# Output projection in four groups of 512 columns with seven-product steps, and two weight sums as one operation

## The chip, the cores and the metric

The kernel runs on one core of a Trainium2 chip. The metric is the device time of one execution in microseconds (us). PE is the matrix engine, DVE the vector engine (VectorE), ACT the scalar engine (ScalarE), POOL GpSimd, SP the queue that issues most loads.

## What is computed

One layer of an encoder for 256 tokens with 2048 features: a gated linear attention mixer, its output projection, a squared-ReLU MLP and a last normalization. Cut to what matters here:

```python
h = x
o = ...                                   # attention, normalized by head, 256 x 2048
h = h + (o * silu(r)) @ w_out             # w_out 2048 x 2048: the output projection
a = relu(rmsnorm(h, mlp_norm) @ w_up)     # w_up 2048 x 8192
h = h + (a * a) @ w_down                  # w_down 8192 x 2048
return rmsnorm(h, final_norm)
```

All inputs are float32.

## The kernel before

**Products in three terms.** Each float32 weight tile is loaded into `raw`, copied by ScalarE to a rounded part `hi` (float32r, L118, `copy_hi`), and VectorE subtracts that from the tile to give `lo` (L131 in `parts`, L165 in `weights`). The activations are kept in two parts in the same way (`oth` and `otl` for the mixer's output, `hh` and `hl` for h). A product is then hi x hi + hi x lo + lo x hi, three matmuls of 128x128 by 128x256. The tokens make two tiles of 128 (`NT` = 2).

**Buffers.** `hi` and `lo` come from five slots each, `raw` from six buffers. ScalarE and VectorE run ahead of PE until the slots are full, and then wait for PE to free one. PE, ScalarE and VectorE each take their instructions in order; the order within an engine is set when the program is built, by a planner that runs the kernel's own order and moves side work (`side`, `pump`) to given steps. `issue_after` pins one instruction behind another in that order.

**The output projection before** is two calls of `natural` (L176 is its matmul, through `halves`), one for each half of 1024 columns of w_out. A call has 16 steps, one for each 128 rows of w_out: one load of 128x1024, one `hi`, one `lo`, and 24 matmuls into four banks (two token tiles by two halves of 512). After a call `add_h` (L640) adds the banks to h.

**Transposes.** The mixer's output `on` and h are turned by PE in bursts of eight transposes of 128x128 (`turn`, L595), four feature tiles each; ScalarE (L600) and VectorE (L601) then take the two parts out of the banks. Bursts one and two of `on` lie in the pass before the projection, three and four in the projection's first half; one and two of h lie in its second half, three and four in the first steps of the MLP.

**Rows at another offset.** After each burst the next step uses rows whose first half lies at another offset in its buffer: `EVEN` = (5, 6) are the two feature tiles concerned, `place_o` gives their places, `xe` holds such copies of x, and `even_at` puts these two tiles at the steps behind the bursts. In the MLP, `even` names the steps whose weights have a gap between their halves (`gap` in `weights`).

**Steps by sums in the MLP.** The down projection works in steps of 256 rows by 512 columns. Split in 2x2 blocks, such a step needs eight block products, or seven of sums of blocks: `forms` makes eight blocks of the activations (four plain, S1 to S4 sums), and the weights' four blocks are replaced in `raw` by sums. One of the weight sums comes with the load: GpSimd's queue loads a block with an accumulating DMA (L938). Three operations of VectorE make the rest in place (L961, L962, L963). So a step has two lots of weights: the loaded blocks (L131, 768 columns) and the sums (L1002, 1024 columns). Four banks collect the products; `combine` (L1043) adds and subtracts them at the end. `by_sums` says which steps are done so: 112 of 120, the last eight loads of w_down aside.

**The order of PE.** In the MLP, `in_order` pins each lot of matmuls behind the one before it.

Of the kernel before, what the change touches and what calls it, by code (L numbers as in the profile page):

```python
# [68 lines left out]
def tile_gla_mlp(ctx, tc, x, xt, cols, w_vg, w_in, w_gate, w_out, w_up, w_down, final_norm, out):  # L69
# [516 lines left out]
                nc.scalar.activation(s, acc[t][c], AF.Silu, scale=r1[:, t : t + 1])  # L586
                nc.vector.tensor_tensor(on[:, t, lo : lo + 512], on[:, t, lo : lo + 512], s, op=ALU.mult)

    def turn(src, row, gain, q):

        bs = [aux_bank(), aux_bank()]
        for i in range(4):
            kt, b, o = 4 * q + i, bs[i // 2], i % 2 * T
            for t in range(NT):
                nc.tensor.transpose(b[:, o + t * P : o + (t + 1) * P], src[:, t, kt * P : (kt + 1) * P], ident)  # L595
        for i in range(4):
            kt, b, o = 4 * q + i, bs[i // 2], i % 2 * T
            s = b[:, o : o + T].rearrange("p (t s) -> p t s", t=NT)
            dh, dl = row(kt)
            nc.scalar.activation(dh, s, AF.Copy, scale=gain(kt))  # L600
            nc.vector.scalar_tensor_tensor(dl, s, gain(kt), dh.bitcast(F32), op0=ALU.mult, op1=ALU.subtract)  # L601
# [4 lines left out]
    oth, otl = (big.tile([P, KT * T + 192], F32R, tag="B", name="ot" + i) for i in "hl")  # L606

    def place_o(kt):
# [6 lines left out]
    def row_o(kt, t):  # L615
        o, d = place_o(kt)
        return [a[:, o + t * d : o + t * d + P] for a in (oth, otl)]

# [8 lines left out]
    side.extend(turns(on, turned_o, gain_o, 0))  # L627
# [5 lines left out]
    side.extend(turns(on, turned_o, gain_o, 2))  # L633
    hs = const.tile([P, NT, 4], F32, name="hs")

    def add_h(acc, c0):
        for c in range(2):
            for t in range(NT):
                lo = c0 + 512 * c
                nc.vector.tensor_tensor(h[:, t, lo : lo + 512], acc[t][c], h[:, t, lo : lo + 512], op=ALU.add)  # L640

    def ssq_h(c0):
        for t in range(NT):
            for c in range(2):
                lo = c0 + 512 * c
                sq = tmp.tile([P, 512], F32, tag="t512", name="sq", bufs=1)
                nc.scalar.activation(sq, h[:, t, lo : lo + 512], AF.Square, accum_out=hs[:, t, lo // 512 : lo // 512 + 1])

    acc = natural(row_o, rows(w_out, 0), G, HALF, order=even_at(2, 4))
    flush()  # L650
    add_h(acc, 0)
# [3 lines left out]
    turned_h = lambda kt: [a[:, kt, :].rearrange("p (t s) -> p t s", t=NT) for a in (hth, htl)]  # L655
    side.extend(turns(h, turned_h, g2, 0))
    side.append(lambda: ssq_h(0))
    acc = natural(row_o, rows(w_out, G), G, HALF, order=even_at(2, 4))
    flush()
    add_h(acc, G)  # L660
    r2 = const.tile([P, NT], F32, name="r2")

    def scale2():
        ssq_h(G)
# [6 lines left out]
    def scale2_row():  # L671

        b = psum_bank(others[-1], "row")
        for t in range(NT):
            d = free_work[:, t * P : (t + 1) * P]
            nc.vector.tensor_scalar(d, ident, r2[:, t : t + 1], None, op0=ALU.mult)
            nc.tensor.matmul(b[:, t * P : (t + 1) * P], ones, d, start=True, stop=True)
        nc.scalar.copy(r2row, b[:, :T])


    side.extend([nothing] * 2 + [lambda: turn(h, turned_h, g2, 2), scale2] + [nothing] * 4)
    side.append(lambda: (turn(h, turned_h, g2, 3), scale2_row()))

    S3, S1, S2, S4, A12, A11, A22, A21 = range(8)
    KP = MR // P // 2
    GROUPS = D // GT
# [21 lines left out]
    firsts, others = list(acc_free)[:2], list(acc_free)[2:]  # L711
    free = deque([*firsts, *aux_free, *others])

    @contextmanager
    def in_order():
        with ExitStack() as order:
            if ordered[0] and last_mm[0]:
                order.enter_context(tc.issue_after(last_mm[0]))
            yield
        last_mm[0] = newest[0]  # L720

    def matmul(o, x, w, first, last):
        newest[0] = nc.tensor.matmul(o, x, w, start=first, stop=last, skip_group_check=True).ins  # L723

    def up():
        ended = deque()
        n_steps = [0]

        def piece():

            if ended:
                with tc.issue_after(last_lo[0].ins), tc.issue_after(last_hi[0].ins):
                    ended.popleft()()

                if n_steps[0] == UPS:
                    last_end[0], last_sum[0] = (i or j for i, j in zip(newest_form, (last_end[0], last_sum[0])))

        for m in range(ROUNDS):
            for q in range(MR // GT):
                taken = [free.popleft() for _ in range(2)]  # L740
                acc = [psum_bank(i, "up") for i in taken]
                even = ((1, 4), (0,))[q] if m == 0 else (6,) if (m, q) in ((ROUNDS // 2 - 1, 0), (ROUNDS - 1, 1)) else ()
# [12 lines left out]

    def up_step(acc, c0, kp, even):

        w = pair_of(w_up, kp, c0, even)

        def products(i, n):
            for j in range(GT // P):
                k = 1 - j % 2
                o = acc[j // 2][:, k * T : (k + 1) * T]
                for a in ((hth, htl), (hth,))[n]:

                    matmul(
                        o, w[n][:, i, j * P : (j + 1) * P], a[:, 2 * kp + i],  # L770
                        kp == i == n == 0 and a is hth and j % 2 == 0, kp == KT // 2 - 1 and n == 1,
                    )

        for i in range(2):
            with in_order():
                products(i, 0)
            if 2 * kp + i < KT - 1:
                pump()
        yield

        with in_order():
            for i in (1, 0) if kp in even else (0, 1):
                products(i, 1)

# [37 lines left out]
    def forms(m, kp, s):  # L822
        f = form
        on_act(nc.scalar.activation(
            f[:, A12:].rearrange("p (t i) s -> p i t s", t=2), s.rearrange("p i (t s) -> p i t s", t=2), AF.Square
        ))
        if True in ways_of(m, kp):
            sub = lambda o, x, y: on_vector(nc.vector.tensor_tensor(o, x, y, op=ALU.subtract))
            sub(f[:, S3 : S1 + 1], f[:, A21:].to_broadcast([P, 2, P]), f[:, A11 : A22 + 1])
            sub(f[:, S2], f[:, A11], f[:, S1])  # L830
            sub(f[:, S4], f[:, A12], f[:, S2])

    def form_parts(m, kp, act):
        ways = ways_of(m, kp)
# [34 lines left out]
    two = lambda bank: bank.rearrange("p (f s) -> p f s", f=2)  # L869

    def begin(k, g):
        i = free.popleft()
# [19 lines left out]
    def down(passes):  # L892
# [7 lines left out]
        for n, (m, g) in enumerate(passes):  # L900
# [12 lines left out]
            for kp in range(KP):  # L913
# [3 lines left out]

                def products(n, these, w, banks=banks, last=last):

                    with in_order():  # L920
# [33 lines left out]
                if by_parts:  # L954
                    these = (P16, 0, at(A11), block(1)), (B32, T, at(A12), block(3)), (B32, 0, at(S4), block(2))
                    u = raw.rearrange("p (f s) -> p f s", f=4)
                    tt = nc.vector.tensor_tensor


                    with tc.issue_after(last_lo[0].ins):  # L960
                        tt(u[:, 2], u[:, 0], u[:, 2], op=ALU.add)  # L961
                        tt(u[:, 1], u[:, 2], u[:, 1], op=ALU.subtract)  # L962
                        last_sum[0] = tt(u[:, 3], u[:, 2], u[:, 3], op=ALU.add).ins  # L963
                else:
                    these = [
                        (k, 0, at(f[i]), block(2 * i, 2))
# [73 lines left out]
    def combine(g):  # L1040
# [4 lines left out]
        def put(t):  # L1045
# [139 lines left out]
```

## Time and profile before

| | |
|---|---|
| Median of three runs | 1048.59 us (1048.42 to 1048.8) |
| Profiled execution | 1048.66 us, span from first to last instruction 1046.9 us |
| Granted PE clock, mean | 0.999 |
| Pass before the projection, end | 287.7 us from the start of the span |
| Output projection | 287.7 to 378.6 us |
| MLP | 378.6 us to the end |

How to read the rows below. The page's first part gives each engine's busy time, share of the span and number of instructions. A row of windows has, for a stretch of time, each engine's busy time and (x) count of instructions, the granted clock of PE, the share of the DMA engines that was in use, and GB/s. A row of groups has line, engine, operation, output and inputs with shapes, count, busy time and mean duration in ns of one, then the engine's idle time before them and what ended it. A row of the timeline has start, time from the first start to the last end, engine, line, operation, and how many instructions were merged. PE's matmuls are pipelined: one lasts 0.28 us, but the next begins long before that.

### The profile page before, as it was taken

The numbers are of one execution on the slowest core, as the hardware profiler recorded it, in microseconds if no ns is written. First come the engines' busy times: TensorE is split into PE (matmuls) and PEld (weight loads), VectorE is DVE, ScalarE is ACT, GpSimd is POOL, SyncE is SP. The second block draws the span as 40 slices with busy tenths as digits, with TensorE's granted clock in tenths as the row PEclk, the third lists the DMA queues.
The fourth block names the chain that finished last, engine by engine and source line by source line (L and its number), as shares of the span: only waits on it lengthen the run. The fifth ranks groups of instructions, "written<-read, shape, count | busy, mean of one in ns | idle before, by whom it ended". The sixth has DMA issues, their size and how long they took to land. (4 is left out here: it accounts for less than half of the span.)

```text
span 1046.9 us, 23145 instructions
## 1 busy us (share of the span) xinstructions
PE 1038.5 (99%) x9094; PEld 1038.2 (99%) x9094; DVE 843.9 (81%) x1225; ACT 703.9 (67%) x1045; POOL 110.1 (11%) x151
## 2 busy tenths in 40 slices
PE   9999999999999999999999999999999999999997
PEld 9999999999999999999999999999999999999997
DVE  5768654656465566889999999999999999999887
ACT  6785544546455455678678678778778777777785
POOL 0000000010000001111111111121211111211100
PEclk9999999999999999999999999999999999999999
DMA  9957665556656666688888887888888888887772
GB/s 337 326 175 215 192 198 165 158 145 180 200 180 184 186 216 193 166 223 226 228 237 229 230 249 210 245 235 224 238 234 227 243 235 229 229 229 223 232 244 88
DMA packets 112717, 225.21 MB, mean 215 GB/s; under 512 B 10288, under 2 KB 25264, under 8 KB 112480
## 3 DMA queue, kind: packets, MB, share of 16 engines
q1 hardware_dynamic: 95808, 207.39, 63.8%
q0 software_dynamic: 16128, 14.69, 9.4%
q10 hardware_dynamic: 672, 1.66, 0.4%
q8 instruction: 71, 1.16, 0.4%
q14 instruction: 38, 0.31, 0.1%
HBM read 221.60 MB, written 2.10 MB: 214 GB/s over the span
## 5 line engine op out<-in xcount | busy, mean ns | idle before, releaser
L118 ACT CAST hi<-raw 128x768 fp32r<-128x768 f32 (+4 forms) x610 | 490.1, 846 | 280.5 <-PE acc L176 105.0
L131 DVE TENSOR_TENSOR lo<-raw,hi 128x768 fp32r<-128x768 f32 (+3 forms) x226 | 241.9, 1072 | 123.7 <-ACT hi L118 121.2
L723 PE MATMUL acc<-hi,act 128*128 128x256 f32 x1696 | 247.8, 276 | 0.0
L723 PE MATMUL up<-hh,hi 128*128 128x256 f32 x1024 | 238.9, 276 | 0.0
L723 PE MATMUL up<-hl,hi 128*128 128x256 f32 x1024 | 238.8, 276 | 0.0
L165 DVE TENSOR_TENSOR lo<-raw,hi 128x1024 fp32r<-128x1024 f32 x160 | 194.7, 1219 | 30.5 <-ACT hi L118 30.2
L723 PEld LDWEIGHTS acc<-hi,act 128*128 128x128 f32 x1696 | 217.7, 188 | 0.0
L723 PEld LDWEIGHTS up<-hl,hi 128*128 128x128 f32 x1024 | 192.2, 188 | 0.0
L723 PEld LDWEIGHTS up<-hh,hi 128*128 128x128 f32 x1024 | 192.2, 188 | 0.0
L938 POOL DMA_DIRECT2D raw<-in_w_down x112 | 98.3, 878 | 516.2 <-DMA raw<-in_w_down 208.0
L1002 DVE TENSOR_TENSOR lo<-raw,hi 128x1024 fp32r<-128x1024 f32 x112 | 136.4, 1218 | 1.6 <-ACT hi L118 1.0
L723 PE MATMUL up<-hh,lo 128*128 128x256 f32 x1024 | 137.0, 276 | 0.0
L723 PE MATMUL acc<-lo,act 128*128 128x256 f32 x848 | 134.0, 276 | 0.0
L723 PEld LDWEIGHTS up<-hh,lo 128*128 128x128 f32 x1024 | 125.7, 188 | 0.0
L723 PEld LDWEIGHTS acc<-lo,act 128*128 128x128 f32 x848 | 113.4, 188 | 0.0
L176 PE MATMUL acc<-hi,xA 128*128 128x256 f32 (+1 forms) x728 | 105.5, 279 | 0.0
L176 PEld LDWEIGHTS acc<-hi,xA 128*128 128x128 f32 x728 | 94.2, 189 | 0.1
L176 PE MATMUL acc<-lo,xA 128*128 128x256 f32 (+1 forms) x364 | 60.7, 278 | 0.0
L176 PEld LDWEIGHTS acc<-lo,xA 128*128 128x128 f32 x364 | 50.3, 188 | 0.0
L961 DVE TENSOR_TENSOR raw<-raw 128x256 f32<-128x256 f32 x112 | 47.4, 423 | 2.9
L962 DVE TENSOR_TENSOR raw<-raw 128x256 f32<-128x256 f32 x112 | 47.4, 423 | 2.8
L219 PE MATMUL acc<-xA,hi 128*128 128x256 f32 x288 | 49.2, 276 | 0.0
(159 smaller groups left out, 1201.2 us busy)
## 6 DMA issues: line engine op xcount, KB each, us to landing
raw<-in_w_up SPq DMA_DIRECT2D x128, 512.0 KB, 4.5
raw<-in_w_down SPq DMA_DIRECT2D x224, 256.0 KB, 4.5
raw<-in_w_in SPq DMA_DIRECT2D x80, 512.0 KB, 3.8
raw<-in_w_out SPq DMA_DIRECT2D x32, 512.0 KB, 3.7
raw<-in_w_down POOLq DMA_DIRECT2D x112, 128.0 KB, 5.2
raw<-in_w_down SPq DMA_DIRECT2D x16, 512.0 KB, 4.9
raw<-in_w_vg SPq DMA_DIRECT2D x14, 520.0 KB, 8.9
h<-in_x SPq DMA_DIRECT2D x4, 512.0 KB, 7.1
```

The lines of the kernel that those rows point to most:

```text
L118: last_hi[0] = nc.scalar.copy(to, raw)
L131: last_lo[0] = nc.vector.tensor_tensor(lo[:, s], raw[:, s], hi[:, s].bitcast(F32), op=ALU.subtract)
L165: last_lo[0] = nc.vector.tensor_tensor(to[1], dst, to[0].bitcast(F32), op=ALU.subtract)
L176: nc.tensor.matmul(o[:, m], x, w[:, m], start=first and c == 0, stop=last, skip_group_check=True)
L219: nc.tensor.matmul(o, u[:, i, s], m, start=kt == 0 and n == 0 and j % 2 == 0, stop=kt == KT - 1 and n == 2, skip_group_check=True,)
L723: newest[0] = nc.tensor.matmul(o, x, w, start=first, stop=last, skip_group_check=True).ins
L938: nc.gpsimd.dma_start(out=raw[:, :T], in_=src[:, 0, T:], accum_op=ALU.add)
L961: tt(u[:, 2], u[:, 0], u[:, 2], op=ALU.add)
L962: tt(u[:, 1], u[:, 2], u[:, 1], op=ALU.subtract)
L1002: last_lo[0] = nc.vector.tensor_tensor(to[1][:, :G], u, to[0][:, :G].bitcast(F32), op=ALU.subtract)
```

## The change

**The output projection** is done by a new function, `out_group`, for each of four groups of 512 columns, in eight steps of 256 rows, in the order of row pairs 3, 0, 2, 1, 4, 7, 5, 6. Pairs 0, 1 and 7 (`FORMED`) are done by sums as in the MLP, 12 steps of 32; the others in plain form, 24 matmuls each. For these three pairs `turn_pair` makes the eight blocks of activations, in two parts, from the transposed bank. The loads are two of 128x512 and one accumulating one for a step by sums, else one of 128x2x512. h is copied into a group's two banks ahead of it (`begin_out`), and two more banks collect sums; at a group's end, VectorE combines these in four operations (into `comb`) and writes h from the two banks and `comb`. The bursts three and four of `on` are done together, in group 0, burst n of h in group n for 1 to 3, all between the second and the third step of a group, ahead of pair 2; the last burst of h stays in the MLP. The rows at another offset are now those of pair 2 (`BOTH` = feature tiles 4 and 5). A second lot of matmuls of a step by sums (`pending`) comes after the next step's.

**Weight sums:** `weight_sums` makes them in two VectorE operations in place of three, the second over two blocks at once, in the projection and in the MLP. Signs differ, and those of the activations' sums (`form_sums`) and of `combine` follow; `form_sums` has three operations as before.

**Order:** `in_order` becomes `then_mm`, which pins PE's lots from the projection on, and in the MLP's first steps too.

The diff, cut to its core:

```diff
+    def form_sums(f, tt):
+        tt(f[:, S3], f[:, A21], f[:, A11], ALU.subtract)
+        tt(f[:, S2 : S1 + 1], f[:, A22 : A22 + 1].to_broadcast([P, 2, P]), f[:, 0::7], ALU.add)
+        tt(f[:, S4], f[:, A12], f[:, S2], ALU.subtract)
+
+    def weight_sums(u):
+        nc.vector.tensor_tensor(u[:, 2], u[:, 0], u[:, 2], op=ALU.subtract)
+        return nc.vector.tensor_tensor(u[:, 1::2], u[:, 1::2], u[:, 2:3].to_broadcast([P, 2, T]), op=ALU.subtract)
...
+    def turn_pair(kp, bank, gain, to):
+        raw_form = raw_forms[kp == 1]
+        for i in range(2):
+            s = bank[:, i * T : (i + 1) * T].rearrange("p (t s) -> p t s", t=NT)
+            nc.scalar.activation(raw_form[:, A12 + 1 - i :: 2], s, AF.Copy, scale=gain(2 * kp + i))
+        form_sums(raw_form, lambda o, x, y, op: nc.vector.tensor_tensor(o, x, y, op=op))
+        nc.scalar.copy(to[0], raw_form)
+        nc.vector.tensor_tensor(to[1], raw_form, to[0].bitcast(F32), op=ALU.subtract)
...
-        e = EVEN[0]
-        if kt in EVEN:
+        e = BOTH[0]
+        if kt in BOTH:
...
-    acc = natural(row_o, rows(w_out, 0), G, HALF, order=even_at(2, 4))
...
-    acc = natural(row_o, rows(w_out, G), G, HALF, order=even_at(2, 4))
...
+        for step, kp in enumerate(order):
+            by = kp in summed
+            raw = raw_tile()[:, : 2 * GT]
...
+            w = parts(raw, 2 * GT, slots(), [(T * by, 2 * GT)])
+            if by:
...
+                products([(p16, 0, at(A11), block(1)), (banks[0], T, at(A12), block(3)), (banks[0], 0, at(S4), block(2))], w)
+                u = raw.rearrange("p (f s) -> p f s", f=4)
+                with tc.issue_after(last_lo[0].ins):
+                    weight_sums(u)
+            else:
+                for t, i in ((0, 0), (0, 1), (1, 0), (1, 1)):
+                    products([(banks[t], 0, row_o(2 * kp + i, t), block(2 * i, 2))], w, step == len(order) - 1 and i == 1)
+            if pending:
+                pending()
+                pending = None
+            if step in between:
+                with tc.issue_after(last_hi[0].ins), tc.issue_after(last_lo[0].ins), then_mm():
+                    between[step]()
...
+    ORDER = (3, 0, 2, 1, 4, 7, 5, 6)
+    out_group(0, ORDER, FORMED, {
+        1: lambda: (turn(on, turned_o, gain_o, 2), turn(on, turned_o, gain_o, 3, forms_o, spare_out(0))),
+        3: lambda: begin_out(1),
+    })
...
+        out_group(g, ORDER, FORMED, {
+            1: lambda: turn(h, turned_h, g2, g - 1), 4: lambda: ssq_h(g - 1),
+            **({3: lambda: begin_out(g + 1)} if g + 1 < GROUPS else {}),
+        })
...
-                even = ((1, 4), (0,))[q] if m == 0 else ...
+                even = ((4,), (0,))[q] if m == 0 else ...
...
-                        tt(u[:, 2], u[:, 0], u[:, 2], op=ALU.add)
-                        tt(u[:, 1], u[:, 2], u[:, 1], op=ALU.subtract)
-                        last_sum[0] = tt(u[:, 3], u[:, 2], u[:, 3], op=ALU.add).ins
+                        last_sum[0] = weight_sums(u).ins
...
-            tt(2, 1, 2, ALU.subtract), tt(0, 0, 2, ALU.subtract), lambda: put(0),
-            tt(1, 2, 3, ALU.subtract), tt(0, 0, 3, ALU.add), lambda: put(1),
+            tt(2, 1, 2, ALU.add), tt(0, 0, 2, ALU.subtract), lambda: put(0),
+            tt(1, 2, 3, ALU.add), tt(0, 0, 3, ALU.subtract), lambda: put(1),
```

More of the change, by code (lines that the diff above doesn't have):

```diff
@@ L587, in gate_out, with turn @@
                 nc.vector.tensor_tensor(on[:, t, lo : lo + 512], on[:, t, lo : lo + 512], s, op=ALU.mult)
-    def turn(src, row, gain, q):
-        bs = [aux_bank(), aux_bank()]
+    S3, S2, S1, S4, A12, A11, A22, A21 = range(8)
+    def form_sums(f, tt):
[5 more added lines that the diff above has]
+        return nc.vector.tensor_tensor(u[:, 1::2], u[:, 1::2], u[:, 2:3].to_broadcast([P, 2, T]), op=ALU.subtract)
+    FORMED = (0, 1, 7)
+    in_forms = lambda a: a.rearrange("p (f s) -> p f s", f=8)
+    raw_forms = [in_forms(some[:, 4:6].rearrange("p a b -> p (a b)")), in_forms(mid.tile([P, G], F32, tag="db", name="form"))]
+    def turn_pair(kp, bank, gain, to):
[6 more added lines that the diff above has]
+        nc.vector.tensor_tensor(to[1], raw_form, to[0].bitcast(F32), op=ALU.subtract)
+    def turn(src, row, gain, q, forms_of=None, banks=None):
+        bs = banks or [aux_bank(), aux_bank()]
         for i in range(4):
@@ L594, in turn @@
             for t in range(NT):
[L595 to L601, printed above, removed]
+                newest[0] = nc.tensor.matmul(
+                    b[:, o + t * P : o + (t + 1) * P], src[:, t, kt * P : (kt + 1) * P], ident, is_transpose=True,
+                    start=i % 2 == t == 0, stop=i % 2 == t == 1, skip_group_check=True,
+                ).ins
+        for kp in (2 * q, 2 * q + 1):
+            if forms_of and kp in FORMED:
+                turn_pair(kp, bs[kp - 2 * q], gain, forms_of(kp))
+                continue
+            for kt in (2 * kp, 2 * kp + 1):
+                i = kt - 4 * q
+                b, o = bs[i // 2], i % 2 * T
+                s = b[:, o : o + T].rearrange("p (t s) -> p t s", t=NT)
+                dh, dl = row(kt)
+                nc.scalar.activation(dh, s, AF.Copy, scale=gain(kt))
+                nc.vector.scalar_tensor_tensor(dl, s, gain(kt), dh.bitcast(F32), op0=ALU.mult, op1=ALU.subtract)
     acc = natural(lambda kt, t: (plain_x if kt == EVEN[1] else row_x)(kt, t), rows(w_in, 4 * KEYW), G, HALF, order=even_at(0, 6))
@@ L606, in tile_gla_mlp, with forms_o @@
     oth, otl = (big.tile([P, KT * T + 192], F32R, tag="B", name="ot" + i) for i in "hl")
+    of_pairs = big.tile([P, 4 * G + 64], F32R, tag="C", name="of")[:, OFF:-16].rearrange("p (b i f s) -> p b i f s", b=2, i=2, f=8)
+    BOTH = (4, 5)
+    def forms_o(kp):
+        if kp < 2:
+            return [of_pairs[:, kp, i] for i in range(2)]
+        return [a[:, OFF : OFF + G].rearrange("p (f s) -> p f s", f=8) for a in (oth, otl)]
     def place_o(kt):
-        e = EVEN[0]
-        if kt in EVEN:
+        e = BOTH[0]
+        if kt in BOTH:
             return e * T + 64 + (kt - e) * (T + 64), P + OFF
@@ L615, in row_o @@
     def row_o(kt, t):
+        if kt // 2 in FORMED:
+            return [a[:, (A11, A21)[t] - kt % 2] for a in forms_o(kt // 2)]
         o, d = place_o(kt)
@@ L625, in turns, with begin_out, spare_out @@
         return [f for q in (q0, q0 + 1) for f in (nothing, lambda q=q: turn(src, row, gain, q))]
-    side.extend(turns(on, turned_o, gain_o, 0))
+    two = lambda a: a.rearrange("p (f s) -> p f s", f=2)
+    out_banks = {}
+    def begin_out(g):
+        for t in range(NT):
+            out_banks[g, t] = bank = psum_bank(out_ids[2 * (g % 2) + t])
+            nc.scalar.copy(bank, h[:, t, g * GT : (g + 1) * GT])
+    def spare_out(g):
+        return [psum_bank(out_ids[2 * (1 - g % 2) + t], "aux") for t in range(NT)]
+    side.extend([nothing, lambda: turn(on, turned_o, gain_o, 0, forms_o)])
+    side.extend([nothing, lambda: turn(on, turned_o, gain_o, 1, forms_o)])
+    side.extend([nothing] * 6 + [lambda: begin_out(0)])
+    r_banks = list(acc_free)
+    out_ids = r_banks[4:] + r_banks[:4]
     acc = natural(row_x, rows(w_in, 5 * KEYW), G, HALF, order=even_at(2, 4))
@@ L649, in tile_gla_mlp, with then_mm @@
-    acc = natural(row_o, rows(w_out, 0), G, HALF, order=even_at(2, 4))
-    flush()
-    add_h(acc, 0)
-    hth, htl = (big.tile([P, KT, T], F32R, tag="A" + i, name="h" + i, bufs=1) for i in "hl")
+    GROUPS = D // GT
+    comb = some[:, 0:3].rearrange("p a b -> p (a b)").rearrange("p (f s) -> p f s", f=6)
+    @contextmanager
+    def then_mm():
+        with ExitStack() as order:
+            if last_mm[0]:
+                order.enter_context(tc.issue_after(last_mm[0]))
+            yield
+        last_mm[0] = newest[0]
@@ new lines, in ssq_h @@
+    def ssq_h(g):
+        for t in range(NT):
+            sq = tmp.tile([P, GT], F32, tag="t512", name="sq", bufs=1)
+            nc.scalar.activation(sq, h[:, t, g * GT : (g + 1) * GT], AF.Square, accum_out=hs[:, t, g : g + 1])
+    ORDER = (3, 0, 2, 1, 4, 7, 5, 6)
+    newest[0] = None
+    out_group(0, ORDER, FORMED, {
+        1: lambda: (turn(on, turned_o, gain_o, 2), turn(on, turned_o, gain_o, 3, forms_o, spare_out(0))),
+        3: lambda: begin_out(1),
+    })
+    hth, htl = (big.tile([P, KT, T], F32R, tag="A" + i, name="h" + i, bufs=1) for i in "hl")
@@ L656, in tile_gla_mlp @@
-    side.extend(turns(h, turned_h, g2, 0))
-    side.append(lambda: ssq_h(0))
-    acc = natural(row_o, rows(w_out, G), G, HALF, order=even_at(2, 4))
-    flush()
-    add_h(acc, G)
     r2 = const.tile([P, NT], F32, name="r2")
     def scale2():
-        ssq_h(G)
+        ssq_h(GROUPS - 1)
         ms2 = st.tile([P, NT], F32, name="ms2")
@@ L669, in scale2, with scale2_diagonals, last_turn @@
             rsqrt(r2[:, t : t + 1], ms2[:, t : t + 1])
-    def scale2_row():
+    def scale2_diagonals():
+        for t in range(NT):
+            nc.vector.tensor_scalar(free_work[:, t * P : (t + 1) * P], ident, r2[:, t : t + 1], None, op0=ALU.mult)
+    def last_turn():
         b = psum_bank(others[-1], "row")
[L674 to L677, printed above, removed]
+        with then_mm():
+            for t in range(NT):
+                c = slice(t * P, (t + 1) * P)
+                newest[0] = nc.tensor.matmul(b[:, c], ones, free_work[:, c], start=True, stop=True).ins
+        with then_mm():
+            turn(h, turned_h, g2, 3)
         nc.scalar.copy(r2row, b[:, :T])
-    side.extend([nothing] * 2 + [lambda: turn(h, turned_h, g2, 2), scale2] + [nothing] * 4)
-    side.append(lambda: (turn(h, turned_h, g2, 3), scale2_row()))
-    S3, S1, S2, S4, A12, A11, A22, A21 = range(8)
+    side.extend([nothing] * 3 + [scale2, nothing, scale2_diagonals] + [nothing] * 2 + [last_turn])
     KP = MR // P // 2
-    GROUPS = D // GT
     work = mid.tile([P, 2 * G + T], F32, tag="qt", name="work")
@@ L774, in up_step @@
         for i in range(2):
-            with in_order():
+            with then_mm():
                 products(i, 0)
@@ L779, in up_step @@
         yield
-        with in_order():
+        with then_mm():
             for i in (1, 0) if kp in even else (0, 1):
@@ L918, in products @@
                 def products(n, these, w, banks=banks, last=last):
-                    with in_order():
+                    with then_mm():
                         for k, o, a, c in these:
```

82 lines of the change are left out of this document (56 added, 26 removed).

## Prediction

> **What bounds the kernel now.** I read the page first, then who waited for whom on PE (one wait in the whole run), then the windows, with their counts of matmuls.
>
> ```profile
> span 1046.9 us, 23145 instructions
> PE 1038.5 (99%) x9094; PEld 1038.2 (99%) x9094; DVE 843.9 (81%) x1225; ACT 703.9 (67%) x1045; POOL 110.1 (11%) x151
> ```
> ```profile
> PE aux L252 <- DVE ones L249: 1.1, 1, 1.1
> ```
> ```profile
> 287.70:333.10 45.40, 45.40 (x402) 45.40 (x401) 25.26 (x29) 21.16 (x26) 0.00 (x0) 1.00 0.60 186
> 333.10:378.60 45.50, 45.50 (x403) 45.50 (x402) 25.30 (x29) 23.51 (x34) 0.00 (x0) 1.00 0.66 197
> 500.00:600.00 100.00, 100.00 (x885) 100.00 (x884) 96.56 (x146) 76.05 (x115) 17.52 (x20) 1.00 0.84 231
> ```
> The first two windows are the two halves of the output projection, the third is the MLP. PE is busy for all of each, at granted clock 1.00, so the time is a count of matmuls times their spacing. VectorE is at 56% in the projection and at 97% in the MLP: it is hidden, but in the MLP with little to spare. What PE pays for a matmul and for a burst of transposes:
>
> ```profile
> 287.71 0.62 PE L176 MATMUL acc<-hi,oth 128*128 128x256 f32 x4
> ```
> ```profile
> 338.58 1.04 PE L595 MATMUL aux<-ident,h 128*128 128x128 f32 x8
> 339.37 0.72 PE L176 MATMUL acc<-hi,oth 128*128 128x256 f32 x4
> 339.93 0.64 PE L176 MATMUL acc<-lo,oth 128*128 128x256 f32 x4
> 340.41 0.64 PE L176 MATMUL acc<-hi,otl 128*128 128x256 f32 x4
> 340.89 0.28 PE L176 MATMUL acc<-hi,oth 128*128 128x256 f32 x1
> ```
> ```profile
> 378.56 0.28 PE L723 MATMUL up<-hh,hi 128*128 128x256 f32 x1
> ```
> A burst with the 12 matmuls behind it takes 340.89 - 338.58 = 2.31 us. The projection runs from 287.71 to 378.56, 90.85 us, with 768 matmuls and four bursts. Solving both: 113.3 ns a matmul, and 0.95 us for a burst above its 12 matmuls' normal time. After a burst the next 12 run at 120 ns (0.48 us for four), then 113 again.
>
> **The change, part by part.**
>
> *Matmuls.* A plain step of 256 rows of w_out by 512 columns has 2 rows x 2 token tiles x 3 terms x 2 halves = 24 matmuls. A step by sums has 7 products x 3 terms = 21. Twelve of 32 are by sums: 12 x 3 = 36 fewer, and the built program's PE list has just that (9026 for 9062). 36 x 113.3 ns = **-4.08 us**, all of it on the path. The Trainium skill ("TensorE: Matmul & The Clock Gate", section "Back-to-back issue gap") puts the warm gap at N/2.4 + 2.5 ns, which makes 109 ns, an estimate, for 256 columns; by it the term would be 3.9 us, but the trace has 113.
>
> *Transposes.* 64 in both.
>
> ```profile
> L595 PE MATMUL aux<-ident,h 128*128 128x128 f32 x32 | 4.1, 273 | 0.0
> ```
> Eight in a row take 1.04 us, the last one's own 0.27 included, so seven spacings are 0.77 and one is 0.11. Group 0 has 16 in one burst, so there are seven bursts for eight; of the eighth, eight spacings of 0.11 remain: 0.95 - 0.87 = **-0.08 us**. The third turn of h moves from the MLP into group 3, with its four ScalarE and four VectorE operations; both places are under PE. In the MLP the gap layout of step 1 goes with it.
>
> *VectorE in the projection.* This was 56% busy and becomes nearly full, so here a new wait could come. Rows by form:
>
> ```profile
> L131 DVE TENSOR_TENSOR lo<-raw,hi 128x1024 fp32r<-128x1024 f32 x94 | 115.0, 1224 | 98.9 <-ACT hi L118 98.9
> L131 DVE TENSOR_TENSOR lo<-raw,hi 128x768 fp32r<-128x768 f32 x112 | 106.7, 953 | 17.3 <-ACT hi L118 14.9 <-PE up L723 1.8 <-DMA raw<-in_w_down 0.2
> L961 DVE TENSOR_TENSOR raw<-raw 128x256 f32<-128x256 f32 x112 | 47.4, 423 | 2.9
> L828 DVE TENSOR_TENSOR work<-work 128x128 f32<-128x128 f32 x60 | 17.1, 285 | 0.3
> L601 DVE SCALAR_TENSOR_TENSOR hl<-aux,colt,hh 128x256 fp32r<-128x256 f32 x16 | 7.2, 480 | 1.1 <-ACT hh L600 0.8
> L640 DVE TENSOR_TENSOR h<-acc,h 128x512 f32<-128x512 f32 x8 | 5.1, 684 | 3.1 <-PE acc L176 3.1
> ```
> One operation is not in the trace, the fused sum of two 128x256 blocks. Below it is one such block (0.42), above it both (0.85); I take 0.68, the row with as many elements.
>
> Groups 1 to 3 each have on VectorE 8 lo's of 1024 (five plain steps, three of sums), 3 of 768, 3 first and 4 combining sums of 256, 3 fused sums and 2 additions into h of 512, 4 parts of the turn: 9.8 + 2.9 + 2.9 + 3.4 + 1.9 = 20.9 us. PE has 183 matmuls and a burst: 20.74 + 0.95 = 21.7 us. The start is group 0. The gating before it ends thus:
>
> ```profile
> 286.32 2.63 ACT L586 ACTIVATE some<-acc,r 128x512 f32<-128x512 f32 x4
> ```
> ```profile
> 287.41 2.49 DVE L587 TENSOR_TENSOR on<-on,some 128x512 f32<-128x512 f32 x4
> ```
> so VectorE is free at 289.90, 2.2 us into the group, and with weights of four slots already cut, as before. From there to the last addition into h the built order gives it 8 lo's of 1024 (the new forms of pair 7 among them), 3 of 768, 8 sums of 256, 5 operations of 512, 6 parts of turns, 2 of 128: 9.8 + 2.9 + 3.4 + 3.4 + 2.9 + 0.6 = 23.0 us. Group 1's transposes need that addition. PE comes to them after group 0 (183 matmuls, 20.74, and 16 transposes, 0.95 + 0.87) and 33 matmuls of group 1 (3.74): 26.3 us in, so VectorE has 24.1 us for 23.0.
>
> To this comes one exposed hand-over: VectorE's fused sum, two ScalarE copies, VectorE's lo. For pair 7 nothing stands between them in VectorE's order (1.2 us idle, two copies of 0.6, with the next steps' lo's queued behind and PE behind those), for pair 1 two parts of the turn cover most of it (0.3 left). By full durations a group then needs 22.4 us against 21.7. Yet operations overlap at their ends:
>
> ```profile
> 503.13 0.95 DVE L131 TENSOR_TENSOR lo<-raw,hi 128x768 fp32r<-128x768 f32 x1
> 504.12 0.43 DVE L961 TENSOR_TENSOR raw<-raw 128x256 f32<-128x256 f32 x1
> 504.58 0.42 DVE L962 TENSOR_TENSOR raw<-raw 128x256 f32<-128x256 f32 x1
> 504.92 0.42 DVE L963 TENSOR_TENSOR raw<-raw 128x256 f32<-128x256 f32 x1
> 505.26 1.22 DVE L165 TENSOR_TENSOR lo<-raw,hi 128x1024 fp32r<-128x1024 f32 x1
> 506.39 1.22 DVE L1002 TENSOR_TENSOR lo<-raw,hi 128x1024 fp32r<-128x1024 f32 x1
> 507.53 0.42 DVE L828 TENSOR_TENSOR work<-work 128x256 f32<-128x256 f32 x1
> 507.86 0.95 DVE L131 TENSOR_TENSOR lo<-raw,hi 128x768 fp32r<-128x768 f32 x1
> ```
> Starts are 1.13 us apart for a duration of 1.22, 0.34 for 0.42. At 0.085 us less for each operation, a group (27 of them) needs 20.1 us, and group 0's stretch (32) 21.8, the exposed 1.5 us included. I take **0 us** of stall, between 0 and the 0.7 us in each of three groups and 0.4 in group 0 by full durations, 2.5 us.
>
> *ScalarE, banks and queues.* ScalarE's added work a group (two copies that begin the next group's banks, two that read the sums' banks, three more pieces of weights) lies in an engine that was 52% busy in the second window. PE's first product into a sums' bank waits for the copy out of it; those copies stand a plain step and more ahead (24 matmuls of step 7, 24 of the next step 0: 5.4 us). SP issues 44 loads for 32 and POOL 12 accumulating ones, behind nothing but each other. In the MLP the same pair
>
> ```profile
> raw<-in_w_down SPq DMA_DIRECT2D x224, 256.0 KB, 4.5
> raw<-in_w_down POOLq DMA_DIRECT2D x112, 128.0 KB, 5.2
> ```
> (4.5 and 5.2 us to landing) runs at 84% DMA share with PE never waiting; here the share was 60 to 66%. All taken at 0; if the cover went, a late accumulation would stop VectorE in order, and is then part of the rival below.
>
> *MLP.* 112 times two sums become one operation. PE waits for nothing there, so a gain is excluded. A loss is not: ScalarE's first copy needed L962 alone and now needs the fused sum, 0.68 - 0.42 = 0.26 us later. A step pair on PE is 24 + 21 matmuls, 5.10 us; VectorE's loop above is 507.86 - 503.13 = 4.73 us. Taken at **0**; the upper end stands with the rivals. The last 46 VectorE and all PE instructions of the tail are in the same order.
>
> Sum: 1046.9 - 4.08 - 0.08 = 1042.7 us of span. The profiled execution took 1048.66 us, 1.76 more than its span and 0.07 above the median of 1048.59. From the median: 1048.59 - 4.16 = 1044.4; with a tenth for small hand-overs, **1044.5 us**.
>
> **Rivals.**
>
> *A. VectorE becomes the bound in the projection.* For it: 20.9 us in a 21.7 us group, with h's addition and the transposes in strict order behind it. Against it: the overlap, and the idle time of the same chain in the MLP,
> ```profile
> L1002 DVE TENSOR_TENSOR lo<-raw,hi 128x1024 fp32r<-128x1024 f32 x112 | 136.4, 1218 | 1.6 <-ACT hi L118 1.0
> ```
> where another operation stands between. By full durations it gives back 2.5 us: 1047.0 (half of it: 1045.7).
>
> *B. The fused sums slow the MLP, slower than before.* Place: each of 112 steps, between the fused sum and ScalarE's copy. VectorE's idle share in the MLP window is 3.44 of 100 us, 0.175 a step pair. If the whole 0.26 us went into its loop and the loop set the pace, 0.085 x 112 = 9.5 us would be lost: 1054. It decides only where more than 0.175 us a step is uncovered. Against it: L165 and L1002 stand between the two, and ScalarE still waits for PE to free slots (31.1 us in this row), so both engines run ahead of PE.
> ```profile
> L118 ACT CAST hi<-raw 128x768 fp32r<-128x768 f32 (+4 forms) x610 | 490.1, 846 | 280.5 <-PE acc L176 105.0 <-DVE raw L962 70.1 <-PE up L723 31.1
> ```
>
> *C. PE keeps the slower spacing after a burst.* It did so once, between two bursts and beyond:
> ```profile
> 181.45 1.10 PE L176 MATMUL acc<-hi,xE 128*128 128x256 f32 x8
> 182.39 0.63 PE L176 MATMUL acc<-lo,xE 128*128 128x256 f32 x4
> ...
> 191.48 0.64 PE L176 MATMUL acc<-hi,xe_gt 128*128 128x256 f32 x4
> 191.96 0.62 PE L176 MATMUL acc<-hi,xA 128*128 128x256 f32 x4
> 192.42 0.62 PE L176 MATMUL acc<-lo,xA 128*128 128x256 f32 x4
> ```
> 118 ns a matmul until the rows that are kept at another offset (xe_gt) had been used, then 113 to 115. In the new code pair 2 follows every burst and its two rows (BOTH) have that offset, so 113 should return. If it didn't, 651 further matmuls of the projection (732 less the 33 ahead of the first burst and the 48 that are slow anyway) at 6.7 ns more are 4.4 us: 1048.9.
>
> *D. The change does less than it says:* excluded for PE's count by the built order.
>
> **How the numbers follow.** Forecast 0.70, with a range of its own of 1043.9 to 1045.3. A 0.15, B 0.05, C 0.05; 0.05 for a tail or start that shifts by itself, to either side. About 0.2%, 2.1 us, is what a measurement of this kernel can tell from no change, so faster means below 1046.5. The forecast and over half of A lie there: 0.81. Within: the rest of A, most of C: 0.12. Slower: B and the rest of C: 0.07. The range takes in A's bound and leaves out B and C: 1043.5 to 1047.0.
>
> **What would show it.** Right: the projection, from PE's last matmul on xE to its first into `up`, takes 4 x 183 x 0.1133 + 1.82 + 3 x 0.95 = 87.6 us, PE waits for nothing in it, and the matmuls behind pair 2 stand in rows of four that take 0.62. A: PE waits for VectorE's h or lo inside the groups. B: PE waits at L856 in the MLP. C: they take 0.63 or 0.64. I would be wrong altogether if PE showed gaps at the groups' starts of a microsecond each.

## The result and the profile after

| | before | after |
|---|---|---|
| Median | 1048.51 us (4 runs, 1048.24 to 1048.8) | 1059.88 us (4 runs, 1059.77 to 1060.14) |
| Ratio | | 1.0107, 95% interval 1.0092 to 1.0121 |
| Span of the profiled execution | 1046.9 us | 1058.1 us, granted clock 0.999 |

The change made the kernel 11.4 us slower; 4.1 us faster was forecast. The page after:

```profile
span 1058.1 us, 23161 instructions
PE 1049.9 (99%) x9058; PEld 1049.1 (99%) x9058; DVE 876.5 (83%) x1171; ACT 722.0 (68%) x1088; POOL 119.5 (11%) x163
```

PE has 36 instructions fewer and yet 11.4 us more of busy time, so the matmuls must stand further apart somewhere. The view of waits on PE has the same single row as before (1.1 us at the start). The windows of after, the first one the output projection, the others pieces of the MLP:

```profile
287.66:375.31 87.65, 87.65 (x775) 87.65 (x774) 78.84 (x111) 63.75 (x105) 7.88 (x9) 1.00 0.69 201
450.00:500.00 50.00, 50.00 (x444) 50.00 (x443) 46.94 (x59) 37.37 (x57) 6.93 (x8) 1.00 0.79 215
550.00:600.00 50.00, 50.00 (x427) 50.00 (x426) 47.22 (x61) 37.42 (x58) 8.65 (x10) 1.00 0.78 219
625.00:675.00 50.00, 50.00 (x443) 50.00 (x442) 47.04 (x63) 37.17 (x58) 8.66 (x10) 1.00 0.80 223
700.00:800.00 100.00, 100.00 (x851) 100.00 (x850) 94.52 (x123) 75.47 (x116) 17.36 (x20) 1.00 0.82 227
```

The projection took 87.65 us. In the MLP, 444 matmuls in 50 us are 113 ns each; 427 in 50 and 851 in 100 are 117 to 118 ns each, with PE "100% busy" and the clock at 1.00 in both. Of the 490 us from 500 to 990, before and after:

```profile
500.00:990.00 490.00, 490.00 (x4325) 490.00 (x4324) 469.87 (x695) 378.06 (x573) 81.56 (x93) 1.00 0.83 232
```
```profile
500.00:990.00 490.00, 490.00 (x4189) 489.90 (x4188) 461.91 (x590) 367.06 (x559) 79.74 (x92) 1.00 0.81 225
```

136 matmuls fewer at 113.3 ns are 15.4 us lost; less the 4.2 us won elsewhere that is 11.2, the difference of the spans. PE's timeline in after shows where the first of these stretches begins:

```profile
519.92 0.28 PE L856 MATMUL up<-hh,hi 128*128 128x256 f32 x1
520.03 0.28 PE L856 MATMUL up<-hl,hi 128*128 128x256 f32 x1
520.15 0.28 PE L856 MATMUL up<-hh,hi 128*128 128x256 f32 x1
520.26 0.28 PE L856 MATMUL up<-hl,hi 128*128 128x256 f32 x1
520.38 0.68 PE L856 MATMUL acc<-hi,act 128*128 128x256 f32 x4
520.89 1.10 PE L856 MATMUL up<-hh,lo 128*128 128x256 f32 x8
521.83 0.63 PE L856 MATMUL acc<-hi,act 128*128 128x256 f32 x4
```

Starts are 0.113 us apart up to 520.38. That group of four took 0.68 instead of 0.62: inside it PE was 0.05 us late, too little for the view of waits. From then on four take 0.63, 118 ns each, until the gap step (a step in `even`, whose weights have a gap between their halves) at 616 us; a second such stretch runs from 680 to about 997. In all some 3500 matmuls of the MLP have the longer spacing, against 36 before (those right behind a burst left out). What PE waited for at 520 was ScalarE's copy of the summed weights:

```profile
518.88 0.68 DVE L598 TENSOR_TENSOR raw<-raw 128x512 f32<-128x512 f32 x1
519.64 1.88 ACT L118 CAST hi<-raw 128x512 fp32r<-128x512 f32 x3 [1.80 <-PE acc L856]
```

The fused sum (L598) ends at 519.56; the first of the three copies in this row starts at 519.64 and ends at 520.26, and the group at 520.38 needs it. (At 680 PE was late for VectorE's L131, which ended at 679.92: another place in the same loop.) VectorE, then ScalarE, of after, in the second stretch:

```profile
757.83 0.42 DVE L597 TENSOR_TENSOR raw<-raw 128x256 f32<-128x256 f32 x1
758.17 0.28 DVE L961 TENSOR_TENSOR work<-work 128x128 f32<-128x128 f32 x1
758.37 0.69 DVE L598 TENSOR_TENSOR raw<-raw 128x512 f32<-128x512 f32 x1
758.97 1.22 DVE L165 TENSOR_TENSOR lo<-raw,hi 128x1024 fp32r<-128x1024 f32 x1
760.40 1.23 DVE L1126 TENSOR_TENSOR lo<-raw,hi 128x1024 fp32r<-128x1024 f32 x1 [0.21 <-ACT hi L118]
```
```profile
759.22 1.14 ACT L118 CAST hi<-raw 128x512 fp32r<-128x512 f32 x2 [1.76 <-PE acc L856]
```

Here the fused sum ends at 759.06, the two copies run from 759.22 to 760.36, and L1126 needs both. Without them it would have begun at about 760.1, 1.13 us after L165's start; VectorE stands still, 0.21 us by the row, which counts from L165's end at 760.19. The rows of the copies name PE as what ended ScalarE's wait, but the copies follow the sum: in 105 of the 112 steps of after the first copy starts 0.03 to 0.17 us after L598's end, and in 104 of the 112 steps of before by as much after L962's. In before the copies of the step that the prediction quoted stood thus:

```profile
505.17 1.14 ACT L118 CAST hi<-raw 128x512 fp32r<-128x512 f32 x2 [2.76 <-DVE raw L962]
```

They ended at 506.31, and L1002 began at 506.39: the cover was just used up in this step, 0.08 us was spare. The groups of VectorE show the sum of it, before 1.6 us idle ahead of L1002 in 112 steps, after ten times that ahead of the same operation (L1126):

```profile
L1126 DVE TENSOR_TENSOR lo<-raw,hi 128x1024 fp32r<-128x1024 f32 x112 | 137.3, 1226 | 16.9 <-ACT hi L118 11.5 <-PE acc L856 0.6
L598 DVE TENSOR_TENSOR raw<-raw 128x512 f32<-128x512 f32 x124 | 85.7, 691 | 3.1
```

### The profile page after: what moved, and what is told of

Same layout as the page of the kernel before. It is cut to its first block, busy times and chain, and to the rows that moved or that the text cites. A ratio compares the mean times of both kernels' runs of the same rounds, so it can differ in the third digit from the quotient of the medians.

```text
span 1058.1 us, 23161 instructions
## 1 busy us (share of the span) xinstructions
PE 1049.9 (99%) x9058; PEld 1049.1 (99%) x9058; DVE 876.5 (83%) x1171; ACT 722.0 (68%) x1088; POOL 119.5 (11%) x163
## 5 line engine op out<-in xcount | busy, mean ns | idle before, releaser
L118 ACT CAST hi<-raw 128x512 fp32r<-128x512 f32 (+4 forms) x634 | 499.3, 833 | 279.1 <-PE acc L176 65.4
L131 DVE TENSOR_TENSOR lo<-raw,hi 128x768 fp32r<-128x768 f32 (+3 forms) x226 | 238.1, 1058 | 84.3 <-ACT hi L118 81.7
L856 PE MATMUL acc<-hi,act 128*128 128x256 f32 x1696 | 252.8, 279 | 0.0
L856 PE MATMUL up<-hh,hi 128*128 128x256 f32 x1024 | 243.8, 278 | 0.0
L856 PE MATMUL up<-hl,hi 128*128 128x256 f32 x1024 | 243.7, 279 | 0.0
L856 PEld LDWEIGHTS acc<-hi,act 128*128 128x128 f32 x1696 | 221.4, 188 | 0.1
L165 DVE TENSOR_TENSOR lo<-raw,hi 128x1024 fp32r<-128x1024 f32 x160 | 194.8, 1220 | 27.1 <-ACT hi L118 26.8
L856 PEld LDWEIGHTS up<-hl,hi 128*128 128x128 f32 x1024 | 192.4, 188 | 0.0
L856 PEld LDWEIGHTS up<-hh,hi 128*128 128x128 f32 x1024 | 192.3, 188 | 0.0
L1126 DVE TENSOR_TENSOR lo<-raw,hi 128x1024 fp32r<-128x1024 f32 x112 | 137.3, 1226 | 16.9 <-ACT hi L118 11.5
L856 PE MATMUL up<-hh,lo 128*128 128x256 f32 x1024 | 139.6, 278 | 0.0
L856 PE MATMUL acc<-lo,act 128*128 128x256 f32 x848 | 136.4, 279 | 0.0
L856 PEld LDWEIGHTS up<-hh,lo 128*128 128x128 f32 x1024 | 128.1, 188 | 0.0
L856 PEld LDWEIGHTS acc<-lo,act 128*128 128x128 f32 x848 | 115.1, 188 | 0.0
L598 DVE TENSOR_TENSOR raw<-raw 128x512 f32<-128x512 f32 x124 | 85.7, 691 | 3.1
L597 DVE TENSOR_TENSOR raw<-raw 128x256 f32<-128x256 f32 x124 | 52.5, 424 | 3.0
```

Of the source, the lines that this page charges most:

```text
L118: last_hi[0] = nc.scalar.copy(to, raw)
L131: last_lo[0] = nc.vector.tensor_tensor(lo[:, s], raw[:, s], hi[:, s].bitcast(F32), op=ALU.subtract)
L165: last_lo[0] = nc.vector.tensor_tensor(to[1], dst, to[0].bitcast(F32), op=ALU.subtract)
L597: nc.vector.tensor_tensor(u[:, 2], u[:, 0], u[:, 2], op=ALU.subtract)
L598: return nc.vector.tensor_tensor(u[:, 1::2], u[:, 1::2], u[:, 2:3].to_broadcast([P, 2, T]), op=ALU.subtract)
L1126: last_lo[0] = nc.vector.tensor_tensor(to[1][:, :G], u, to[0][:, :G].bitcast(F32), op=ALU.subtract)
```

## The experiments

**Theory 1**, as first put: the fused sum delays ScalarE's first copy; PE is late once by some 50 ns; every matmul after that takes 118 ns until a step in the gap layout. Rivals are numbered from 2 on.

| run | median us | ratio to before, 95% interval |
|---|---|---|
| e1: after, three sums in the MLP | 1044.04 | 0.9956 (0.9942 to 0.9969) |
| e2: before, fused sums in the MLP | 1066.01 | 1.0167 (1.0153 to 1.0181) |
| e3: after, three sums, block 1 last | 1063.89 | 1.0148 (1.0134 to 1.0162) |
| e4: after, 12 more gap steps | 1059.07 | 1.0095 (1.0081 to 1.0109) |
| e5: before, VectorE delayed once | 1071.47 | 1.0230 (1.0214 to 1.0245) |
| e6: after, copies by blocks 0, 2 and 1, 3 | 1044.21 | 0.9961 (0.9948 to 0.9973) |
| e9: e5 and a gap step after the delay | 1059.8 | 1.0109 (1.0092 to 1.0126) |

e7, e8 and e10 leave matmuls out and were run once each.

### Which part of the change is it: e1, e2, e3

e1 puts three operations back in the MLP:

```diff
-                        last_sum[0] = weight_sums(u).ins
+                        tt = nc.vector.tensor_tensor
+                        tt(u[:, 2], u[:, 0], u[:, 2], op=ALU.subtract)
+                        tt(u[:, 1], u[:, 1], u[:, 2], op=ALU.subtract)
+                        last_sum[0] = tt(u[:, 3], u[:, 3], u[:, 2], op=ALU.subtract).ins
```

> The changed kernel with the MLP's weight sums as three operations again (the new signs kept); the projection is untouched and keeps its fused sums. Theory 1 (in the MLP the fused sum hands ScalarE its first block 0.26 us later, PE is late once by some 50 ns, and every matmul after that takes 118 ns instead of 113 until a step in the gap layout): the first copy is back in time, PE stays at 113 ns through the MLP, 885 matmuls in each 100 us, and the time is what the projection alone should give, 1044.4 us. Rival 2 (the projection's new order, its banks or the changed signs leave the MLP behind): the stretches at 118 ns stay, about 1059 us.

1044.04 us, span 1042.8. Its window has before's count again, and VectorE's idle time is gone:

```profile
500.00:990.00 490.00, 490.00 (x4325) 490.00 (x4324) 469.38 (x697) 378.01 (x572) 80.64 (x93) 1.00 0.83 232
```
```profile
L1129 DVE TENSOR_TENSOR lo<-raw,hi 128x1024 fp32r<-128x1024 f32 x112 | 136.7, 1220 | 1.3 <-ACT hi L118 1.2
```

So the projection, its banks and the signs do no harm; all the loss hangs on the MLP's sums. e2 is the reverse, before with `weight_sums`, `form_sums` and `combine` of after:

```diff
...
-                        tt(u[:, 2], u[:, 0], u[:, 2], op=ALU.add)
-                        tt(u[:, 1], u[:, 2], u[:, 1], op=ALU.subtract)
-                        last_sum[0] = tt(u[:, 3], u[:, 2], u[:, 3], op=ALU.add).ins
+                        last_sum[0] = weight_sums(u).ins
...
```

> The kernel before with only the fused sums, in the MLP, with the signs they need; the projection is that of before. Theory 1: PE is late somewhere and stretches at 118 ns (849 matmuls in 100 us) appear; where they begin is chance, so 1050 to 1064 us. Rival 2 (the projection causes it): no such stretch, 1048.5 us.

1066.01 us, 17.3 above before, a little past the range given. Rival 2 is out. e3 fuses nothing, and makes block 1 last:

```diff
-                        last_sum[0] = weight_sums(u).ins
+                        tt = nc.vector.tensor_tensor
+                        tt(u[:, 2], u[:, 0], u[:, 2], op=ALU.subtract)
+                        tt(u[:, 3], u[:, 3], u[:, 2], op=ALU.subtract)
+                        last_sum[0] = tt(u[:, 1], u[:, 1], u[:, 2], op=ALU.subtract).ins
```

> The changed kernel with three operations in the MLP, but in the order 2, 3, 1, so that the block that ScalarE copies first is complete one operation of 0.34 to 0.42 us later than in the order 2, 1, 3. Nothing is fused. Theory 1 (it is the late first copy that counts): as slow as the changed kernel or slower, 1050 to 1064 us, with stretches at 118 ns. Rival 3 (the fused form of the operation itself does it, by its strided and repeated operands): as with the order 2, 1, 3, 1044.4 us.

1063.89 us. With the same three operations as e1 in another order, 20 us are lost. So no fused operation is needed for the loss: it is enough that the block that is copied first is ready later.

### Is it one late matmul, or the loop: e4, e7, e8

```diff
-                even = ((4,), (0,))[q] if m == 0 else (6,) if (m, q) in ((ROUNDS // 2 - 1, 0), (ROUNDS - 1, 1)) else ()
+                even = ((4,), (0,))[q] if m == 0 else (6,)
```

> The changed kernel, fused sums and all, with the gap layout of step 6 in each round of the MLP and each of its halves from round 1 on, instead of twice: 12 more steps that cost 0.08 us each, 1.0 us, if nothing else follows from them. Theory 1 (a spacing that lasts until the gap layout is used): each stretch at 118 ns ends at the next such step, some 60 us on at most, and 15 us of loss shrink to 3 to 6: 1047 to 1052 us. Rival 4 (each late matmul and each slow stretch comes from what VectorE does just then, no state that lasts): 1060 to 1061 us.

1059.07 us: theory 1 missed by 7 us. PE did return to 113 ns at the gap steps, and some 1390 matmuls had the longer spacing instead of some 3500. But it was late some 45 times instead of four, by up to 0.49 us, and these waits took what the spacing gave back. The span of the profiled execution is 1055.4 us, 12.6 above e1's: 6.5 of it are waits, and about 6 the longer spacing. Its window from 500 to 990 us:

```profile
500.00:990.00 490.00, 488.54 (x4215) 485.28 (x4215) 462.80 (x591) 367.77 (x559) 79.77 (x92) 1.00 0.81 226
```

A pair of steps, one of the up projection and one by sums, has 24 + 21 = 45 matmuls, 5.10 us at 113.3 ns; 4215 are 93.7 pairs of 5.23. So at 113 ns PE outruns its weights. Rival 5 was formed from this: the loop of VectorE and ScalarE itself has become longer than 5.10 us, and the longer spacing, 5.30 us a pair, hides that. e7 (after) and e8 (before) leave out of the MLP one matmul in three, hi weights by lo activations, so that PE never sets the pace:

```diff
-                for a in ((hth, htl), (hth,))[n]:
+                for a in (hth,):
...
-                            for x in a[: 2 - n]:
+                            for x in a[: 1]:
```

> The changed kernel without one matmul in three of the MLP (the term of the high part of the weights with the low part of the activations is left out of the computation), so that PE is far ahead and a pair of steps lasts as long as the loop of VectorE and ScalarE. PE's own time for a pair would be 30 matmuls, 3.4 to 3.55 us. Theory 1 in its narrow form (the loop is fast enough, a single late matmul does it all): a pair still takes under 5.10 us. Rival 5 (the loop itself has become longer than PE's 5.10 us, which the slower spacing of 5.30 us hides): 5.15 to 5.25 us a pair, and the time of the whole about 1045 to 1055 us.

> The kernel before with the same third of the MLP's matmuls left out. Both theories: the loop of VectorE and ScalarE takes less than PE's 5.10 us, 4.75 to 5.0 us a pair; the difference to the changed kernel's loop is what the fused sum costs, at most the 0.26 us of the prediction, by theory 1 in its narrow form 0.1 us or less, by rival 5 0.2 us or more. The whole is 15 to 30 us faster than before.

The windows of e7 and e8, 400 us of the MLP each:

```profile
500.00:900.00 400.00, 336.43 (x2299) 290.02 (x2298) 376.88 (x476) 304.72 (x465) 66.76 (x77) 1.00 0.82 227
```
```profile
500.00:900.00 400.00, 341.08 (x2400) 296.07 (x2398) 390.37 (x581) 315.32 (x480) 70.17 (x80) 1.00 0.86 237
```

A pair is 30 matmuls here, so 2299 are 76.6 pairs of 5.22 us, and 2400 are 80 pairs of 5.00. PE's 5.10 lies between the two. Rival 5 holds: the change lengthened the loop by 0.22 us and made it the bound, and e7's 5.22 us is also what e4 took for a pair with all its matmuls, 5.23. The whole took 1041.73 us (e7, below the 1045 to 1055 expected) and 1021.55 (e8).

### A cure that keeps the fused sum: e6, e10

```diff
-                    for c in (0, GT):
-                        copy_hi(to[0][:, c : c + GT], u[:, c : c + GT])
+                    in_4 = lambda a: a.rearrange("p (f s) -> p f s", f=4)
+                    for c in range(2):
+                        copy_hi(in_4(to[0][:, :G])[:, c :: 2], in_4(u)[:, c :: 2])
...
-                    early = (P57, 0, at(S1), block(0)), (P57, T, at(S3), block(1))
-                    late = (P16, T, at(S2), block(2)), (BX4, T, at(A22), block(3))
+                    early = (P57, 0, at(S1), block(0)), (P16, T, at(S2), block(2))
+                    late = (P57, T, at(S3), block(1)), (BX4, T, at(A22), block(3))
```

> The changed kernel, fused sums kept, but ScalarE's two copies of the summed weights take blocks 0 and 2 first (complete before the fused sum) and 1 and 3 then, and PE takes the four products in that order. VectorE's list of work is that of the changed kernel. Theory 1 (what counts is when ScalarE's first copy may start): that copy now needs only the first, 256 wide sum, 0.34 us earlier than in the kernel before, so PE keeps 113 ns and the time is 1044 us, as with three operations. Rival 3 (the fused operation itself, 0.69 us with repeated operands, is what disturbs): nothing gets better, 1055 to 1062 us.

1044.21 us, as theory 1 had it: with the fused sum in place and its delay of the first copy gone, the loss is gone. VectorE of e6, where L1127 follows L165 with no idle time:

```profile
760.74 0.42 DVE L597 TENSOR_TENSOR raw<-raw 128x256 f32<-128x256 f32 x1
761.19 0.69 DVE L598 TENSOR_TENSOR raw<-raw 128x512 f32<-128x512 f32 x1
761.80 1.22 DVE L165 TENSOR_TENSOR lo<-raw,hi 128x1024 fp32r<-128x1024 f32 x1
762.93 1.22 DVE L1127 TENSOR_TENSOR lo<-raw,hi 128x1024 fp32r<-128x1024 f32 x1
```

e10 is e6 with the edit of e7.

> The changed kernel with fused sums and copies by blocks 0, 2 and 1, 3, and without one matmul in three of the MLP (the same term is left out as in the two such runs before), to read the loop of VectorE and ScalarE: 5.21 us a pair in the changed kernel, 4.99 in the one before. Theory 1, wider (the late first copy is what lengthened the loop): at most 4.99 us, and down to 4.9 since the fused sum saves VectorE 0.08 us. Rival 3 (the fused operation): 5.15 to 5.25.

```profile
500.00:900.00 400.00, 329.33 (x2451) 298.56 (x2451) 393.00 (x510) 331.64 (x492) 70.72 (x82) 1.00 0.88 242
```

2451 matmuls are 81.7 pairs of 4.90 us (the whole: 1005.8 us). The loop is now 0.10 us shorter than before the change. e1 and e6 beat both kernels; their intervals overlap, so no order between them is shown.

### Does the longer spacing last by itself: e5, e9

e5 delays VectorE once, in the kernel before, whose loop keeps up:

```diff
+        if (c0, kp) == (4 * MR, 2):
+            some = tmp.tile([P, 512], F32, tag="t512", name="wait", bufs=1)
+            with tc.issue_after(last_lo[0].ins):
+                nc.vector.memset(some, 0.0)
+                for _ in range(16):
+                    end = nc.vector.tensor_tensor(some, some, some, op=ALU.add)
+            last_sum[0] = end.ins
```

> The kernel before, with 16 additions of 128x512 put in VectorE's way once, in the first half of round 4 of the MLP (some 620 us), nothing else changed and no result touched: PE is made late once by some microseconds (16 of 0.6 us less what the weights are cut ahead). Theory 1 (after a wait PE keeps 118 ns until the gap layout, here at about 984 us): the wait, and 3200 matmuls at 4.5 ns more, 13 to 14 us: 1062 to 1073 us. Rival 4 (no state that lasts): the wait and what VectorE's slack of 0.2 us a pair makes of it, 1 to 10 us, with PE at 113 ns wherever it doesn't wait: 1050 to 1058 us.

e9 has the same delay and this:

```diff
-... in ((ROUNDS // 2 - 1, 0), (ROUNDS - 1, 1)) else ()
+... in ((ROUNDS // 2 - 1, 0), (4, 0), (ROUNDS - 1, 1)) else ()
```

> The delayed kernel before, and one step more in the gap layout, step 6 of the first half of round 4, some 20 us after PE's long wait (8.6 us at 678 us, measured with the delay alone, and 1071.5 us). Theory 1 (the slower spacing is a state of PE that the gap layout ends): PE returns to 113 ns at about 707 us instead of 1002; unless it is late again, 300 us at 118 ns are saved, 11 us: 1060 to 1062 us; with one relapse half way, 1066. Rival 4 (the 118 ns come from something that the delay leaves behind in VectorE, ScalarE or the queues): the gap step changes nothing, 1071 us.

1071.47 and 1059.8 us. PE of e5 after its wait, with the rows at 708 us, then the same of e9, where the gap step lies there:

```profile
686.81 2.08 PE L723 MATMUL up<-hh,lo 128*128 128x256 f32 x8 [8.35 <-DVE lo L165]
688.68 1.05 PE L723 MATMUL acc<-hi,act 128*128 128x256 f32 x4
...
708.97 0.63 PE L723 MATMUL acc<-hi,act 128*128 128x256 f32 x4
```
```profile
708.88 0.62 PE L723 MATMUL acc<-hi,act 128*128 128x256 f32 x4
709.34 1.10 PE L723 MATMUL up<-hh,lo 128*128 128x256 f32 x8
710.27 0.62 PE L723 MATMUL acc<-hi,act 128*128 128x256 f32 x4
```

And both from 800 to 900 us, e5 first:

```profile
800.00:900.00 100.00, 100.00 (x851) 100.00 (x850) 92.02 (x137) 75.97 (x115) 17.08 (x20) 1.00 0.80 227
```
```profile
800.00:900.00 100.00, 100.00 (x885) 100.00 (x884) 95.80 (x146) 78.00 (x119) 16.84 (x20) 1.00 0.84 234
```

For each matmul VectorE's busy time is the same in both (92.02/851 and 95.80/885, 0.108 us) and ScalarE's within 2%. One wait left PE at 118 ns for some 320 us, from 690 to 1008, although nothing made it wait again; one gap step ended that and saved 11.7 us, a little more than was expected. This half of theory 1 stands. A gap step also takes its `lo` products in the other order, and no run tells which of the two it is.

## Why the prediction was wrong

**Matmuls, transposes, projection: right.** 87.65 us measured for 87.6 forecast, no wait, rows of four of 0.62 behind pair 2. Rival A did not happen, and neither did C in the projection. e1, the change without its MLP part, took 1044.04 us for 1044.5.

**VectorE's fused sum: right in size.** 0.691 us for the 0.68 taken.

**MLP "taken at 0": the step that failed.** The delay of the first copy was seen and sized, 0.26 us, and it lengthened the loop by 0.22 (e7, e8). What failed was its cover, in two places. "L165 and L1002 stand between the two" counted L1002 as cover, but L1002 is the operation that waits for the copies: only L165 stood between, and in the step shown 0.08 us was spare. And "VectorE's loop above is 4.73 us" was read from one pair that had one short piece of the activations' work in it; e8 measured 5.00, so the slack to PE's 5.10 was 0.10, not 0.37, and not the 0.175 of rival B either. 0.22 less 0.10 leaves 0.12 us a pair, 13 us in 112 pairs; the window above lost 15.4, the share of the longer spacing included. That is rival B, priced at 9.5 us and given a chance of 0.05.

**Rival C, confined to the projection: wrong place.** The longer spacing came in the MLP, from PE being late by 0.05 us, with no burst near. In this kernel it sets the last few us: a pair at 118 ns takes 5.30 us, over the loop's 5.22. With the spacing cut short by gap steps (e4) the ratio to before, 1.0095, stayed within the interval of after, 1.0092 to 1.0121, so the loop and not the spacing is the first cause here. Where the loop keeps up, the spacing alone cost 11.7 us (e5 against e9). Rival C's price was also misread: its own rows show 118 ns, 4.7 above 113.3, but it was priced at 6.7, the excess of the 120 ns right behind a burst; 651 matmuls at 4.7 are 3.1 us, not 4.4.

**"PE waits at L856 in the MLP" as the sign of B** hardly showed: PE was late four times, by 0.05 to 0.11 us. The sign was the count of matmuls in a window.

Left open: what in PE keeps the spacing. A wait can lead to either one: in e3, PE was late by 0.34 us at 650.5 us and came out of it at 113 ns.

## What to carry over

Making two operations one delays whoever waits for the first of them alone: give the consumer first what is ready first, as e6 does. Cover counts only operations that stand ahead of the waiting one, and a slack is read from the mean over many steps or, better, by taking work off the bound engine and timing the rest. Where an engine is "100% busy" in both kernels, compare its instructions per 100 us.

## What the runs showed of the hardware

- **PE has two spacings at the same granted clock, 1.00:** 113.3 and 118 ns for matmuls of 256 columns. A wait of 0.05 us was followed by the longer one (after, 520.38 us); it stayed for 96 us in after and some 320 us in e5; a step in the gap layout, with its `lo` products in the other order, brought the shorter one back (e9). A wait can do so too (e3, 650.5 us).
- **After 8.35 us without work PE began at half pace:** in e5, eight matmuls in 2.08 us, starts 213 ns apart until 689.7 us, 3 us in all, at a granted clock of 0.50. The Trainium skill ("TensorE: Matmul & The Clock Gate", section "What's actually happening") says that an idle window of about 3.4 us halves PE's clock, and that about as long a busy one brings it back. The trace agrees, with 8.35 us idle and 3 us at half pace. Only e5 and e9 had a wait of that length, and the windows at 118 ns have a granted clock of 1.00, so the 118 ns are not that state.
